# A projection's products with the high halves of the weights all issued ahead of those with the low halves

## The chip, the cores and the metric

The kernel runs on one core of one Trainium2 chip. The metric is device time in microseconds (us) of one execution. The three runs of the kernel before took 1165.89, 1167.34 and 1170.15 us, so the median is 1167.34 us.

## What is computed

The reference chains two transformer-like blocks over 256 tokens of width 1024, in float32. Cut to what matters here:

```python
# first block: 16 meta tokens + 256 tokens
proj = rms_norm(h) @ w_in                    # attention, RWKV and gate columns
merged = sigmoid(gate_sb) * (y_sb @ w_sb_out) + sigmoid(gate_rw) * (y_rw @ w_rw_out)
h = h + merged @ w_out
gate_ffn, up_ffn = split(rms_norm(h) @ w_ffn_in)       # 2 x 2816 columns
h = h + (silu(gate_ffn) * up_ffn) @ w_ffn_out
# second block
mod = silu(c) @ w_ada + b_ada                # shifts, scales and gates
proj = modulated(h) @ w_in_2                 # gated delta rule, HGRN2, gates
x = x + g1 * (concat(oA, oB) @ w_out_2)
x = x + g2 * moe(modulated(x))               # 64 experts, 8 of them for each token
```

All the products with `w_in`, `w_sb_out`, `w_rw_out`, `w_out`, `w_ffn_in`, `w_ffn_out`, `w_in_2` and `w_out_2` are called projections below.

## The kernel before

**Weights.** The weights of the projections are cut into tiles of 128x128 numbers and laid out in the order in which they are used. Eight tiles make a unit (`UNIT = 8`); there are 168 units, counted here from 0. `unit` (L270 to L280) loads a unit by one DMA of 512 KB on SP's queue into a `raw` buffer, and `split` (L322 to L326) then makes two tiles of it: ScalarE (ACT) writes the high half `whi`, a copy in the matmul's reduced float32 (L324), and VectorE (DVE) or, for the 30 units listed in `POOLU`, GpSimd (POOL) subtracts it from `raw` to give the low half `wlo` (L325). The three kinds of tile have three buffers each. `wt` (L285 to L292) hands out one tile's two halves and calls for the unit after it as well (`AHEAD = 1`).

**Products.** The activations are kept as a high and a low half too. Each weight tile takes part in three matmuls that add up in one PSUM tile: high by high, high by low, and low weight by high activation. Every matmul has 256 columns (272 where the meta tokens are included). So a unit has 24 products, 16 of them with `whi` and 8 with `wlo`. `mm3` (L328 to L332) issues the three one behind another; `linear` (L334 to L339) does so for the `kt` tiles of one output tile `m`. `pair` (L341 to L359) holds two output tiles in one PSUM tile and writes the three matmuls out (L352, L357, L358); ffn_in's 22 pairs come from it. `linears` (L361 to L369) with `by_k` takes several output tiles together, one activation tile `k` after another, so that PE can begin while the activations still arrive: the first three tiles of the program (`rw_lo`), the first two of `w_out` (`EARLYM = 2`) and the first two of the second block (`k2`). `mix_half` (L1380 to L1396) does the second output projection.

**Order.** Stages are Python generators whose turns are written in strings of letters (`FIRST`, `MIXER`), and ffn_out (`residual`, L987) advances the loads of `w_ada` (`ada`) between its tiles; these are loaded by SP into `wada` buffers and summed on DVE (L1086). A list scheduler then places the instructions on each engine's queue by dependencies, buffers and its own estimates. Each queue runs in its written order. From about 780 us to the end the kernel runs the experts, with a schedule written by hand in which the projections' code has no part.

**Stages in time.** Up to 330 us: the first block's projections, recurrences, attention, mixing and `w_out` (about 300 us). 330 to 460 us: ffn_in. 460 to 545 us: ffn_out, 8 output tiles of 22 weight tiles each. 545 to about 750 us: the second block's projections and recurrences: the convolution and decay work of the gated delta rule (L1208, L1209, L1217, L1223), the scans of HGRN2 (L1270, L1274), the inverse of the delta rule (`base_inverse`, L393 and L394). Then the router and the experts.

Of the kernel before, what the change touches and what calls it, by code (L numbers as in the profile page):

```python
# [40 lines left out]
UNIT = 8  # L41
# [168 lines left out]
class Ker:  # L210
# [117 lines left out]
    def mm3(self, out, w, x, start, stop):  # L328
# [2 lines left out]
        mm(out, w[0], x[1], start=False, stop=False)  # L331
        mm(out, w[1], x[0], start=False, stop=stop)  # L332

    def linear(self, block, m, kt, x, n, tag="mm"):  # L334

        p = self.psum(tag)
        for k in range(kt):
            self.mm3(p[:, :n], self.wt(block, m * kt + k), x(k), k == 0, k == kt - 1)
        return p[:, :n]  # L339

    def pair(self, block, parts, kt, x, by_k=False):  # L341

        p = self.psum().rearrange("p (a b) -> p a b", b=S)
        steps = [(i, m, k) for i, (m, ks) in enumerate(parts) for k in ks]
        if by_k:
            steps.sort(key=lambda t: t[2])
        mm = self.nc.tensor.matmul
        for n, (i, m, k) in enumerate(steps):
            w, v = self.wt(block, m * kt + k), x(k)
            last = k == parts[i][1][-1]  # L350
            kw = dict(skip_group_check=True)
            a = mm(p[:, i], w[0], v[0], start=(n == 0), stop=False, **kw)  # L352
            if n == 0:
                first = a
            elif k == parts[i][1][0]:
                self.order(a, first)
            mm(p[:, i], w[0], v[1], start=False, stop=False, **kw)  # L357
            mm(p[:, i], w[1], v[0], start=False, stop=last, **kw)  # L358
        return p  # L359

    def linears(self, block, ms, kt, x, n, by_k, tag="mm"):  # L361

        if not by_k:
            return [self.linear(block, m, kt, x, n, tag) for m in ms]
        ps = [self.psum(tag)[:, :n] for _ in ms]
        for k in range(kt):
            for p, m in zip(ps, ms):
                self.mm3(p, self.wt(block, m * kt + k), x(k), k == 0, k == kt - 1)
        return ps  # L369

    def rsqrt(self, out, src, scale, eps, tmp):
# [1008 lines left out]
    def mix_half(self, c):  # L1380

        if not c:
            self.pmix = [self.psum("ax") for _ in range(3)] + [self.psum("mm")]
        yh, yl = self.ymix2
        for m in range(KD):
            p = self.pmix[m // 2][:, m % 2 * S:m % 2 * S + S]
            for k in range(4):
                w = self.wt("w_out2" + "ab"[c], 4 * m + k)
                x = (yh[:, 4 * c + k], yl[:, 4 * c + k])
                mm = self.nc.tensor.matmul  # L1390
                kw = dict(skip_group_check=True)
                mm(p, w[0], x[0], start=(c == 0 and k == 0 and m % 2 == 0), stop=False, **kw)
                mm(p, w[0], x[1], start=False, stop=False, **kw)
                mm(p, w[1], x[0], start=False, stop=(c == 1 and k == 3), **kw)
            if c:
                yield m, p  # L1396

# [782 lines left out]
```

## Time and profile before

| | before |
|---|---|
| three runs | 1165.89, 1167.34, 1170.15 us |
| median | 1167.34 us |
| the profiled execution | 1175.33 us |
| its span | 1173.5 us |
| mean granted TensorE clock | 0.959 of full speed |
| PE busy | 1086.6 us, 93% of the span |
| DVE busy | 682.1 us, 58% |
| ACT busy | 436.8 us, 37% |
| POOL busy | 243.0 us, 21% |

The profiled execution is 8.0 us (0.7%) longer than the median of the runs; its span, from the first to the last instruction that the profile records, is 1.8 us shorter than its own time. PE's 93% is an average over stages with different limits: between 330 and 460 us PE hardly pauses, in the stages before and after it waits for other engines, and from 780 us on it runs beside a DMA stream that is always full. "Idle before" in a row is the time for which the engine stood still ahead of the instruction, and the arrow names what ended that.

### The profile page before, as it was taken

To read this page: it belongs to the slowest core of one execution; us is meant where nothing else is said; L and a number is where in the kernel's file an instruction comes from. 1 tells how busy PE (TensorE), PEld (TensorE's weight loads), DVE (VectorE), ACT (ScalarE), POOL (GpSimd) and SP (SyncE) were. 2 spreads that over 40 slices of the span, in tenths; PEclk is the share of its full clock that TensorE was granted. 3 is DMA by queue.
4 is the path that set the end of the run, shared out by engine and by line. 5 is a ranking of instruction groups with operands and counts; after the bars stand their busy time and mean duration, and the time that the engine had idled before them with its cause. 6 is when DMAs were issued, how large, how long until landed. Compare 5 with 4: busy or idle time off the path is not lost.

```text
span 1173.5 us, 20361 instructions
## 1 busy us (share of the span) xinstructions
PE 1086.6 (93%) x8038; PEld 831.6 (71%) x8038; DVE 682.1 (58%) x1211; ACT 436.8 (37%) x707; POOL 243.0 (21%) x245
## 2 busy tenths in 40 slices
PE   5989899999989999988988999899999999999994
PEld 4889787789979999877988889773444444444441
DVE  5598633346678888877799888522233333333333
ACT  5744433365454444335854645411111111111112
POOL 1261102023312000486472131410000000000000
PEclk9899969999989999998999999799999999999998
DMA  5455511024558898864443504959999999999993
GB/s 174 141 145 176 177 55 37 1 86 166 179 198 298 314 341 302 306 232 145 148 146 127 176 28 174 415 182 344 418 413 392 419 419 419 399 419 418 420 418 139
DMA packets 67495, 290.69 MB, mean 248 GB/s; under 512 B 15984, under 2 KB 17136, under 8 KB 46912
## 3 DMA queue, kind: packets, MB, share of 16 engines
q1 hardware_dynamic: 66528, 287.93, 65.5%
q8 instruction: 66, 1.08, 0.4%
q10 hardware_dynamic: 864, 1.38, 0.3%
q14 instruction: 37, 0.30, 0.1%
HBM read 285.77 MB, written 3.51 MB: 247 GB/s over the span
## 4 chain that ended last, share of the span: by engine, by line
PE 45%; DMA 16%; DVE 11%; issue 4%; ACT 4%; POOL 3%; SPq 0%; POOLq 0%; ACTq 0%; DVEq 0%
DMA er<-in_E_dram 10%; PE bank L1880 10%; PE bank L1908 5%; PE p_b L357 3%; PE p_b L358 3%; PE p_b L352 3%; DMA wada<-in_W_ada_dram 3%; PE acc L1777 3%; PE bank L1840 3%; DMA xa<-in_E_dram 3%; DVE wada L1086 2%; DVE wlo L325 2%; PE p_b L787 2%; ACT k L306 2%; PE p_b L332 2%
## 5 line engine op out<-in xcount | busy, mean ns | idle before, releaser
L324 ACT ACTIVATE whi<-raw 128x1024 fp32r<-128x1024 f32 x168 | 175.5, 1055 | 102.7 <-PE p_b L331 37.0
L325 DVE TENSOR_TENSOR wlo<-raw,whi 128x1024 fp32r<-128x1024 f32 x138 | 178.4, 1299 | 59.5 <-ACT whi L324 55.4
L358 PE MATMUL p_b<-k,wlo 128*128 128x256 f32 x608 | 175.7, 290 | 4.9 <-DVE wlo L325 3.0
L352 PE MATMUL p_b<-k,whi 128*128 128x256 f32 x608 | 176.1, 290 | 3.5 <-ACT k L324 2.3
L357 PE MATMUL p_b<-k,whi 128*128 128x256 f32 x608 | 176.1, 290 | 2.3 <-DVE k L325 2.3
L332 PE MATMUL p_b<-k,wlo 128*128 128x256 f32 (+2 forms) x496 | 144.6, 296 | 13.1 <-DVE wlo L325 9.0
L330 PE MATMUL p_b<-k,whi 128*128 128x256 f32 (+2 forms) x496 | 146.8, 300 | 9.3 <-ACT k L324 4.1
L331 PE MATMUL p_b<-k,whi 128*128 128x256 f32 (+2 forms) x432 | 126.8, 296 | 0.3 <-DVE k L1114 0.3
L358 PEld LDWEIGHTS p_b<-k,wlo 128*128 128x128 f32 x608 | 118.6, 195 | 8.3 <-DVE wlo L325 4.0
L352 PEld LDWEIGHTS p_b<-k,whi 128*128 128x128 f32 x608 | 118.8, 196 | 5.1 <-ACT k L324 2.4
L325 POOL TENSOR_TENSOR wlo<-raw,whi 128x1024 fp32r<-128x1024 f32 x30 | 81.6, 2723 | 196.7 <-ACT whi L324 136.5
L357 PEld LDWEIGHTS p_b<-k,whi 128*128 128x128 f32 x608 | 118.8, 196 | 3.8 <-DVE k L325 2.8
L332 PEld LDWEIGHTS p_b<-k,wlo 128*128 128x128 f32 (+1 forms) x496 | 97.1, 198 | 15.8 <-DVE wlo L325 10.9
L330 PEld LDWEIGHTS p_b<-k,whi 128*128 128x128 f32 (+1 forms) x496 | 97.4, 198 | 14.6 <-ACT k L324 5.1
L1880 PE MATMUL bank<-er,x 128*32 128x512 f32 (+2 forms) x464 | 91.9, 612 | 2.6 <-DMA er<-in_E_dram 2.5
L1908 PE MATMUL bank<-er,k 128*32 128x512 f32 (+2 forms) x488 | 89.9, 595 | 2.6 <-DMA er<-in_E_dram 1.4
L1880 PE MATMUL bank<-er,h 128*32 128x512 f32 (+2 forms) x488 | 87.5, 595 | 0.0
L1828 POOL TENSOR_TENSOR k<-k,masks 128x128 f32<-128x128 f32 (+3 forms) x44 | 17.3, 423 | 335.7 <-DVE y L325 310.8
L331 PEld LDWEIGHTS p_b<-k,whi 128*128 128x128 f32 (+1 forms) x432 | 85.7, 199 | 0.8 <-DVE k L1114 0.6
L1086 DVE SCALAR_TENSOR_TENSOR wada<-wada,crow 128x1024 f32<-128x1024 f32 x48 | 70.9, 1484 | 21.7 <-DMA wada<-in_W_ada_dram 21.6
L1885 ACT ACTIVATE k<-bank 128x256 f32<-128x256 f32 x24 | 9.2, 384 | 195.7 <-PE bank L1880 195.7
L1886 DVE SCALAR_TENSOR_TENSOR k<-k,gs,bank 128x256 f32<-128x256 f32 x24 | 11.5, 481 | 101.9 <-ACT k L1885 101.9
(476 smaller groups left out, 2043.5 us busy)
## 6 DMA issues: line engine op xcount, KB each, us to landing
er<-in_E_dram SPq DMA_DIRECT2D x132, 1024.0 KB, 17.7
raw<-in_W_dram SPq DMA_DIRECT2D x168, 512.0 KB, 3.9
wada<-in_W_ada_dram SPq DMA_DIRECT2D x48, 512.0 KB, 5.5
xa<-in_E_dram SPq DMA_DIRECT2D x24, 1024.0 KB, 12.5
xa<-in_Sh_dram SPq DMA_DIRECT2D x2, 1024.0 KB, 8.3
k<-in_xT_dram SPq DMA_DIRECT2D x4, 272.0 KB, 4.7
dl<-x SPq DMA_DIRECT2D x1, 1024.0 KB
x<-in_xT_dram SPq DMA_DIRECT2D x1, 1024.0 KB
```

The costliest lines, as they stand in the source:

```text
L324: ins = self.nc.scalar.activation(hi, src, AF.Copy)
L325: (engine or self.nc.vector).tensor_tensor(lo, src, hi.bitcast(F32), op=OP.subtract)
L330: mm(out, w[0], x[0], start=start, stop=False)
L331: mm(out, w[0], x[1], start=False, stop=False)
L332: mm(out, w[1], x[0], start=False, stop=stop)
L352: a = mm(p[:, i], w[0], v[0], start=(n == 0), stop=False, **kw)
L357: mm(p[:, i], w[0], v[1], start=False, stop=False, **kw)
L358: mm(p[:, i], w[1], v[0], start=False, stop=last, **kw)
L1086: nc.vector.scalar_tensor_tensor(w, w, 1.0, c, op0=OP.mult, op1=OP.mult, accum_out=self.mod[:, o:o + 1])
L1777: self.nc.tensor.matmul(self.acc[t], w, x, start=t not in self.started, stop=False, skip_group_check=True)
L1880: mm(ph[t], X[:, k, i * 128 + t.start:i * 128 + t.stop], u[:, kk * 512:kk * 512 + 512], start=(k == 0), stop=(k == KD - 1), skip_group_che ...
L1908: nc.tensor.matmul(py[t], q.H[:, k, t], u[:, k * 1024 + c * 512:k * 1024 + c * 512 + 512], start=(k == 0), stop=(k == 1), skip_group_check ...
```

## The change

Within a run of tiles, all the products with `whi` are written first and all the products with `wlo` behind them. A new helper `three` does that for a list of terms. `by_unit` cuts an output tile's `kt` weight tiles at the borders of units, so that in `linear` a run is at most one unit. In `pair` a run is one of the two output tiles (8 weight tiles), or, with `by_k`, both of them together. In `linears` with `by_k` one run holds all the tiles of all the outputs. In `mix_half` a run is 4 tiles. `mm3` stays for the small products outside. No product, load, split or buffer is added or taken away; PE has as many instructions as before. The list scheduler works on the changed program, so the queues of DVE, ACT, POOL and SP differ from before here and there as well.

```diff
+    def three(self, terms, **kw):
+        mm = self.nc.tensor.matmul
+        for out, w, x, start, _ in terms:
+            mm(out, w[0], x[0], start=start, stop=False, **kw)
+            mm(out, w[0], x[1], start=False, stop=False, **kw)
+        for out, w, x, _, stop in terms:
+            mm(out, w[1], x[0], start=False, stop=stop, **kw)
+
+    def by_unit(self, block, tiles):
+        runs = []
+        for t in tiles:
+            u = (self.off[block] + t) // UNIT
+            if not runs or runs[-1][0] != u:
+                runs.append((u, []))
+            runs[-1][1].append(t)
+        return [r for _, r in runs]
+
     def linear(self, block, m, kt, x, n, tag="mm"):
-        p = self.psum(tag)
-        for k in range(kt):
-            self.mm3(p[:, :n], self.wt(block, m * kt + k), x(k), k == 0, k == kt - 1)
-        return p[:, :n]
+        p = self.psum(tag)[:, :n]
+        for run in self.by_unit(block, range(m * kt, m * kt + kt)):
+            self.three([(p, self.wt(block, t), x(t - m * kt), t == m * kt, t == m * kt + kt - 1) for t in run])
+        return p
...
     def pair(self, block, parts, kt, x, by_k=False):
...
+        groups = [steps] if by_k else [[s for s in steps if s[0] == i] for i in range(len(parts))]
...
+        for g in groups:
+            for i, m, k in g:
...
+                mm(p[:, i], w[0], v[1], start=False, stop=False, **kw)
+            for i, m, k in g:
+                w, v = self.wt(block, m * kt + k), x(k)
+                mm(p[:, i], w[1], v[0], start=False, stop=k == parts[i][1][-1], **kw)
...
     def linears(self, block, ms, kt, x, n, by_k, tag="mm"):
...
-        for k in range(kt):
-            for p, m in zip(ps, ms):
-                self.mm3(p, self.wt(block, m * kt + k), x(k), k == 0, k == kt - 1)
+        self.three([(p, self.wt(block, m * kt + k), x(k), k == 0, k == kt - 1) for k in range(kt) for p, m in zip(ps, ms)])
```

**ffn_out, PE, around unit 116.** PE's queue before, in one of ffn_out's output tiles: `whi_5225` and `wlo_5226` are unit 116's halves, `whi_5195` and `wlo_5196` those of unit 115, and `hid_3320` and `hid_3321` the activations' high and low halves.

```order
L330 MATMUL p_b3_5260<-hid_3320,whi_5195 128x256
L331 MATMUL p_b3_5260<-hid_3321,whi_5195 128x256
L332 MATMUL p_b3_5260<-hid_3320,wlo_5196 128x256
L330 MATMUL p_b3_5260<-hid_3320,whi_5225 128x256
L331 MATMUL p_b3_5260<-hid_3321,whi_5225 128x256
L332 MATMUL p_b3_5260<-hid_3320,wlo_5226 128x256
```

The same place after the change:

```order
L339 MATMUL p_b3_5260<-hid_3320,whi_5225 128x256
L340 MATMUL p_b3_5260<-hid_3321,whi_5225 128x256
L342 MATMUL p_b3_5260<-hid_3320,wlo_5226 128x256 x8
L339 MATMUL p_b3_5260<-hid_3320,whi_5275 128x256
L340 MATMUL p_b3_5260<-hid_3321,whi_5275 128x256
```

Before, unit 116's first `wlo` product stood behind two of its `whi` products. Now it stands behind 16 of them.

**ffn_out, DVE, unit 107.** DVE's queue before; `wlo_4897` is unit 107's low half, L1086 sums one 512 KB piece of `w_ada`:

```order
L1055 TENSOR_SCALAR k1_4848<-k1_4848 128x8
L325 TENSOR_TENSOR hid_3321<-k1_4839,hid_3320 128x256
L1086 SCALAR_TENSOR_TENSOR wada_5244,mod_2669<-wada_5244,crow_3389 128x1024
L325 TENSOR_TENSOR wlo_4897<-raw_4894,whi_4896 128x1024
L325 TENSOR_TENSOR wlo_4927<-raw_4924,whi_4926 128x1024
L1086 SCALAR_TENSOR_TENSOR wada_5247,mod_2669<-wada_5247,crow_3389 128x1024
L1086 SCALAR_TENSOR_TENSOR wada_5250,mod_2669<-wada_5250,crow_3389 128x1024
```

And after the change:

```order
L1077 TENSOR_SCALAR k1_4848<-k1_4848 128x8
L325 TENSOR_TENSOR hid_3321<-k1_4839,hid_3320 128x256
L325 TENSOR_TENSOR wlo_4897<-raw_4894,whi_4896 128x1024
L1108 SCALAR_TENSOR_TENSOR wada_5244,mod_2669<-wada_5244,crow_3389 128x1024
L325 TENSOR_TENSOR wlo_4927<-raw_4924,whi_4926 128x1024
L1108 SCALAR_TENSOR_TENSOR wada_5247,mod_2669<-wada_5247,crow_3389 128x1024
L1018 TENSOR_TENSOR x1_79<-p_b3_4851,x1_79 128x256
```

The split of unit 107 now stands ahead of a sum over `w_ada`, and unit 108's ahead of another, where before one sum stood ahead of both.

**Second block, DVE and PE, unit 138.** DVE's queue before, where `wlo_6244` and `wlo_6279` are the low halves of units 138 and 139:

```order
L1208 TENSOR_SCALAR k2_6082<-p_b5_6077,k1_6071 128x128
L1209 TENSOR_SCALAR k2_6083<-p_b5_6077,k1_6071 128x128
L325 TENSOR_TENSOR wlo_6244<-raw_6241,whi_6243 128x1024
L325 TENSOR_TENSOR wlo_6279<-raw_6276,whi_6278 128x1024
L1223 SCALAR_TENSOR_TENSOR k4_6067<-p_b7_6096,k1_6009,k2_6082 128x128 x4
L1208 TENSOR_SCALAR k2_6158<-p_b5_6153,k1_6147 128x128
L1209 TENSOR_SCALAR k2_6159<-p_b5_6153,k1_6147 128x128
```

After the change (L1230, L1231, L1245, L1292 and L1296 are the old L1208, L1209, L1223, L1270 and L1274):

```order
L1230 TENSOR_SCALAR k2_6158<-p_b5_6153,k1_6147 128x128
L1231 TENSOR_SCALAR k2_6159<-p_b5_6153,k1_6147 128x128
L1292 SCALAR_TENSOR_TENSOR k4_6188<-k1_6184,k4_5913 128x256 x4
L325 TENSOR_TENSOR wlo_6244<-raw_6241,whi_6243 128x1024
L1245 SCALAR_TENSOR_TENSOR k4_6067<-p_b7_6174,k1_6009,k2_6158 128x128 x4
L1296 TENSOR_TENSOR k4_5916<-k4_5916,p_b4_6193 128x256
L1296 TENSOR_TENSOR k4_5916<-k4_5916,p_b0_6228 128x256
L325 TENSOR_TENSOR wlo_6279<-raw_6276,whi_6278 128x1024
```

The split of unit 138 has moved from ahead of four L1223 to behind them, behind eight of L1208 and L1209, and behind the four scans. PE's queue at that unit after the change (`whi_6278` is unit 139's high half):

```order
L339 MATMUL p_b3_6333<-k8_5668,whi_6278 128x256
L340 MATMUL p_b3_6333<-k8_5669,whi_6278 128x256
L342 MATMUL p_b1_6263<-k8_5668,wlo_6244 128x256 x4
L342 MATMUL p_b2_6298<-k8_5668,wlo_6244 128x256 x4
L339 MATMUL p_b2_6298<-k8_5668,whi_6278 128x256
```

Ahead of these rows stand the 16 `whi` products of unit 138, so that its first `wlo` product, which before followed two products of the unit, now follows 24 products with `whi`: 16 of its own and 8 of unit 139, which were moved ahead of it.

## Rows read from the trace of the kernel before

**Rows 1.** The page: busy time, share of the span and instructions of PE

```profile
PE 1086.6 (93%) x8038; PEld 831.6 (71%) x8038; DVE 682.1 (58%) x1211; ACT 436.8 (37%) x707; POOL 243.0 (21%) x245
```

**Rows 2.** PE's waits over the span: engine, line, awaited, us in total, times, longest

```profile
PE p_b L332 <- DVE wlo L325: 11.7, 11, 2.5
PE p_b L332 <- POOL wlo L325: 10.8, 5, 3.4
...
PE p_b L358 <- DVE wlo L325: 3.0, 4, 1.7
...
PE p_b L358 <- POOL wlo L325: 1.9, 1, 1.9
```

**Rows 3.** PE's waits in 0:150 (first row), 460:545 (two), 600:665 (two)

```profile
PE p_b L332 <- DVE wlo L325: 4.9, 5, 1.9
...
PE p_b L332 <- POOL wlo L325: 6.7, 3, 3.4
PE p_b L332 <- DVE wlo L325: 2.7, 2, 1.5
...
PE p_b L332 <- POOL wlo L325: 4.0, 2, 2.4
PE p_b L332 <- DVE wlo L325: 3.4, 3, 2.5
```

**Rows 4.** Windows: us, busy of PE, PEld, DVE, ACT, POOL, clock, DMA share, GB/s

```profile
60.00:120.00 60.00, 56.13 (x453) 53.90 (x452) 54.12 (x92) 25.92 (x36) 22.82 (x16) 1.00 0.56 164
460.00:545.00 85.00, 71.32 (x571) 68.91 (x569) 67.17 (x80) 32.32 (x43) 46.56 (x30) 0.96 0.74 258
600.00:665.00 65.00, 55.76 (x434) 54.10 (x433) 63.98 (x126) 35.39 (x47) 22.53 (x13) 0.95 0.46 143
```

**Rows 5.** The page: groups, with busy time and mean ns of one

```profile
L325 DVE TENSOR_TENSOR wlo<-raw,whi 128x1024 fp32r<-128x1024 f32 x138 | 178.4, 1299 | 59.5 <-ACT whi L324 55.4
...
L325 POOL TENSOR_TENSOR wlo<-raw,whi 128x1024 fp32r<-128x1024 f32 x30 | 81.6, 2723 | 196.7 <-ACT whi L324 136.5
```

**Rows 6.** Timeline of PE around 505 us: start, duration, engine, line; idle before

```profile
505.24 0.58 PE L332 MATMUL p_b<-hid,wlo 128*128 128x256 f32 x1 [3.41 <-POOL wlo L325]
505.62 0.41 PE L330 MATMUL p_b<-hid,whi 128*128 128x256 f32 x1
...
508.16 0.28 PE L330 MATMUL p_b<-hid,whi 128*128 128x256 f32 x1
508.28 0.28 PE L331 MATMUL p_b<-hid,whi 128*128 128x256 f32 x1
```

**Rows 7.** Timeline of PE: two more long waits, at 361 and 523 us

```profile
360.95 0.39 PE L358 MATMUL p_b<-k,wlo 128*128 128x256 f32 x1 [1.91 <-POOL wlo L325]
...
361.46 0.42 PE L358 MATMUL p_b<-k,wlo 128*128 128x256 f32 x1
...
523.22 0.39 PE L332 MATMUL p_b<-hid,wlo 128*128 128x256 f32 x1 [2.35 <-POOL wlo L325]
523.45 0.28 PE L330 MATMUL p_b<-hid,whi 128*128 128x256 f32 x1
```

**Rows 8.** Timeline of PE: the early tiles of w_out and k2, last activations

```profile
306.17 0.39 PE L330 MATMUL p_b<-k,whi 128*128 128x256 f32 x1 [1.12 <-ACT k L324]
...
307.33 0.28 PE L330 MATMUL p_b<-k,whi 128*128 128x256 f32 x1
...
553.07 0.35 PE L331 MATMUL p_b<-k,whi 128*128 128x256 f32 x1
```

**Rows 9.** Timeline of DVE (three rows) and PE (one) around unit 138

```profile
583.80 2.35 DVE L325 TENSOR_TENSOR wlo<-raw,whi 128x1024 fp32r<-128x1024 f32 x2
587.33 1.13 DVE L1223 SCALAR_TENSOR_TENSOR k<-p_b,k,k 128x128 f32<-128x128 f32 x4 [1.18 <-POOL k L1217]
...
590.44 4.49 DVE L1270 TENSOR_TENSOR_SCAN k<-k,k 128x256 f32<-128x256 f32 x3
...
587.50 0.28 PE L330 MATMUL p_b<-k,whi 128*128 128x256 f32 x1
```

More of the change, by code (lines that the diff above doesn't have):

```diff
@@ L332, in mm3 @@
         mm(out, w[1], x[0], start=False, stop=stop)
+    def three(self, terms, **kw):
[13 more added lines that the diff above has]
+        return [r for _, r in runs]
     def linear(self, block, m, kt, x, n, tag="mm"):
-        p = self.psum(tag)
-        for k in range(kt):
-            self.mm3(p[:, :n], self.wt(block, m * kt + k), x(k), k == 0, k == kt - 1)
-        return p[:, :n]
+        p = self.psum(tag)[:, :n]
+        for run in self.by_unit(block, range(m * kt, m * kt + kt)):
+            self.three([(p, self.wt(block, t), x(t - m * kt), t == m * kt, t == m * kt + kt - 1) for t in run])
+        return p
     def pair(self, block, parts, kt, x, by_k=False):
         p = self.psum().rearrange("p (a b) -> p a b", b=S)
+        mm = self.nc.tensor.matmul
+        kw = dict(skip_group_check=True)
         steps = [(i, m, k) for i, (m, ks) in enumerate(parts) for k in ks]
@@ L346, in pair @@
             steps.sort(key=lambda t: t[2])
[L347 to L358, printed above, removed]
+        groups = [steps] if by_k else [[s for s in steps if s[0] == i] for i in range(len(parts))]
+        first = None
+        for g in groups:
+            for i, m, k in g:
+                w, v = self.wt(block, m * kt + k), x(k)
+                a = mm(p[:, i], w[0], v[0], start=first is None, stop=False, **kw)
+                if first is None:
+                    first = a
+                elif k == parts[i][1][0]:
+                    self.order(a, first)
+                mm(p[:, i], w[0], v[1], start=False, stop=False, **kw)
+            for i, m, k in g:
+                w, v = self.wt(block, m * kt + k), x(k)
+                mm(p[:, i], w[1], v[0], start=False, stop=k == parts[i][1][-1], **kw)
         return p
@@ L1386, in mix_half @@
             p = self.pmix[m // 2][:, m % 2 * S:m % 2 * S + S]
[L1387 to L1394, printed above, removed]
+            self.three([(p, self.wt("w_out2" + "ab"[c], 4 * m + k), (yh[:, 4 * c + k], yl[:, 4 * c + k]),
+                         c == 0 and k == 0 and m % 2 == 0, c == 1 and k == 3) for k in range(4)], skip_group_check=True)
             if c:
```

## The prediction

> **What bounds the kernel now.** I read the page's busy times first: PE works for 1086.6 us, 93% of the span [rows 1], so a change that only reorders PE's instructions can gain no more than what PE stands still for. The view of PE's waits shows how much of that belongs to the low halves of the weights: 11.7 us in 11 waits and 10.8 us in 5 at L332, 3.0 us in 4 and 1.9 us in 1 at L358 [rows 2], together 27.4 us in 21 waits, 2.3% of the time. Cut by stretch, the larger parts are 4.9 us before 150 us, 6.7 + 2.7 = 9.4 us in ffn_out (460 to 545 us), and 4.0 + 3.4 us between 600 and 665 us [rows 3]. Then the windows, which tell whether PE's wait is the one that ends last there. In ffn_out nobody is full: in 85 us DVE works for 67.2, POOL for 46.6, and the DMA engines for 0.74 of the time. From 600 to 665 us DVE works for 64.0 of 65 us, so PE's waits are DVE's shadow; from 60 to 120 us it works for 54.1 of 60 [rows 4]. From about 780 us on nothing of the change is executed: what is gained before shifts the experts forward as a block.
>
> Why PE waits is seen in one timeline. At 505.24 us the wait of 3.41 us ends at a product with `wlo`, and a product with `whi` follows at once, 0.38 us later [rows 6]: it needed only what was there, and stood in the queue behind the low half. The queue as printed ahead of this text shows that two `whi` products of unit 116 came before it. The low half is ready late because it is the last of a chain, with 1.30 us for DVE's subtraction and 2.72 us for POOL's [rows 5].
>
> **The change, part by part.**
>
> *Cover.* In a run of eight tiles 16 products now precede the first `wlo` one, 14 more than before. At 0.12 us from one start to the next (508.16 to 508.28 [rows 6]) that is 14 x 0.12 = 1.68 us; every wait loses what it has up to that.
>
> *ffn_out.* The three waits on POOL are 3.41 us [rows 6], 2.35 us [rows 7] and the rest of 6.7, 0.99 us; the first two keep 1.73 and 0.67 us. So 9.4 - 2.4 = **7.0 us** go. One unit, 107, serves an output tile with two of its tiles only and has little cover; its split was moved ahead of a sum over `w_ada` on DVE, as the queue shows, and I count it as covered by that. The upper bound is all 9.4 us; the lower is 3.5 us, if SP's loads, which were placed anew among those of `w_ada`, bring back half. I take 7.0 because DVE, POOL and DMA each have a fifth of the stretch or more to spare [rows 4].
>
> *ffn_in.* The one long wait, 1.91 us at 360.95 us [rows 7], loses 1.68: **1.7 us**; PE is the fullest engine there.
>
> *Before 150 us.* 4.9 us at L332 [rows 3] bound it above. DVE is 90% busy from 60 to 120 us [rows 4], and an inverse with a long chain on DVE ends what follows; below, nothing. I take half, **2.5 us**: the rows give DVE a tenth of the time to spare, so neither end is near.
>
> *600 to 665 us.* **Nothing**, for want of a free DVE. Were that cover gone, up to 7.4 us would come back.
>
> *The clock.* After the 3.41 us wait a product lasts 0.41 us where it lasts 0.28 from 508.16 us on; twelve products start between 505.62 and 508.16 us, 0.21 us apart, and then again 0.12 [rows 6]. So 12 x 0.09 = 1.1 us went to the lower of the two clocks (1.2 GHz). A wait of 1.91 us at 360.95 was followed by the lower clock too (0.42 us for the product at 361.46); one of 2.35 us at 523.22 was not, as the next product's 0.28 us tells [rows 7]. Both lowered clocks should be kept up when the waits shrink to 1.7 and 0.2 us: **2.2 us**, with 0 and 2.2 as its ends. The Trainium skill, "TensorE: Matmul & The Clock Gate", section "Loop structure matters more than you think", blames the drop on a long wait between matmuls; read so, only the longest of these waits gives clock back, and the forecast would stand 1.1 us higher. The row at 360.95 us speaks against so strict a reading, and I go by it.
>
> *Runs by `by_k`: a cost.* In the first two tiles of `w_out` the last activation came at 306.17 us, after a wait of 1.12 us, and the next output tile began at 307.33 us [rows 8]. With eight activations and two output tiles, 16 `wlo` products now stand behind it all, where two did: 14 x 0.12 = 1.7 us of work that used to fill the gaps between the activations comes after them. The first pair of k2, whose last activation came at about 553.07 us [rows 8], is the same, and its output feeds the convolution. Each costs 0 (if the deferred products fill gaps further on) to 1.7 us; I take 1.5 each, being near the row with a real wait: **-3.0 us**. For the first three tiles of the program and ffn_in's first pair I take nothing: there the products run behind the activations at the lower clock, so PE has work anyway; at most 1.7 us each.
>
> *DVE's queue at unit 138: a cost.* Before, the splits of units 138 and 139 ran from 583.80 us for 2.35 us, in time that DVE would have lost waiting for POOL until 587.33 us (a wait of 1.18 us remained) [rows 9]. Now 138's is behind that wait, four L1223 (1.13 us), eight L1208 and L1209 (until 590.44 us) and four scans, three of which took 4.49 us [rows 9]. At 1.5 us a scan that is 590.4 + 6.0 + 1.2 = 597.6 us at the latest, and 594 to 595 if the scans run at their fastest. PE comes to the unit at 587.50 us [rows 9] and has 24 `whi` products first, 2.9 us: it will stand still from 590.4 for about 4 to 7 us. What this costs the end is less, since from 600 us on DVE is what ends last: DVE loses the 2.35 us of work that lay in its wait. Between 0 and 7 us I take **-2.35 us**.
>
> *ACT, POOL and SP* issue what they issued before, a high half here or there earlier; nothing, since none of them is near full in any stretch of [rows 4].
>
> **Sum.** 7.0 + 1.7 + 2.5 + 2.2 - 3.0 - 2.35 = 8.05 us. Against the profiled execution, 1175.3 us, that gives 1167.3; it stands 8.0 us above the median of the runs, and on the median I forecast 1167.3 - 8.0 = **1159.3 us**, 0.7% less.
>
> **Rivals.**
>
> *The waits only move.* The low halves come no sooner; where DVE is the limit PE meets them later and as long. Then the early 2.5 us stay out, ffn_out keeps 5 us, only the clock of the 505 us wait comes back (1.1), and unit 138 costs PE its full 7 us: 5 + 1.7 + 1.1 - 3.0 - 7 = -2.2, so 1169.5; with half that cost, 1166. For it speaks DVE's 64.0 of 65 us [rows 4]; against it, that ffn_out, where most of the waiting is, has no full engine. Some 1163 to 1171 us.
>
> *All of it comes back.* If the reordering lets DVE start its chain sooner, the 4.9 us before 150 us and the 7.4 us after 600 us return as well, and unit 138 costs nothing: 8.05 + 2.4 + 7.4 + 2.35 = 20.2 us, 1147 us. Against it: the full DVE.
>
> *Slower: the scheduler defers the splits.* It places a split by when it thinks the low half is needed, and that is now later. On a full DVE a deferred split is a wait of PE's like the 7 us at unit 138. One such unit is already in the sum; it turns the sign when two more of the same price are not absorbed (8.05 - 14 = -6): 1173 us, and 1180 with three. The place is the second block, 580 to 665 us, where splits, scans and the inverse share DVE. Against it: the queues elsewhere show splits moved ahead as often as back.
>
> That the change does nothing is ruled out for PE's order, which is visibly other; it could do nothing for the time, which is the first rival.
>
> **How the numbers follow.** A change of 0.5%, 5.8 us, is about what a measurement of this kernel can tell from none, so faster means below 1161.5 and slower above 1173.2 us. The forecast (1154 to 1164 us) gets 0.47, the first rival 0.30, the full return 0.12, the slower one 0.11. Of the forecast's 0.47, 0.39 lies below 1161.5 us; with the full return that makes 0.51 for faster. The other 0.08 and 0.28 of the first rival give 0.36 for no difference; the slower rival and the upper edge of the first, 0.02, give 0.13 for slower. The range goes from 1149 to 1171 us: below it most of the full return is left out, above it the slower rival.
>
> **What would show it.** In the changed profile: PE's waits for `wlo` in ffn_out down from 9.4 to about 2.4 us, in ffn_in near nothing; no lower clock right behind 361 and 505 us (on the new time axis); a new wait of PE of 4 to 7 us at the first `wlo` product of unit 138; two tails of 16 `wlo` products each with a DVE or POOL consumer behind it; DVE still full between 600 and 665 us with PE's waits of some 7 us left. The experts' stage should begin about 8 us earlier and last as long as before. I am wrong if the waits in ffn_out reappear under another name (the high half, or a load), if the second block takes 5 us or more longer than before, or if the early stages give back nothing.

## The result, and the profile after

The changed kernel takes 1183.42 us, median of 4 runs (1179.35 to 1187.19); the kernel before, run beside it, 1168.74 us (1165.89 to 1172.12, 4 runs). The ratio on record is 1.0115, with a 95% interval of 1.0085 to 1.0144: **slower by 1.2%**. The medians lie 14.7 us apart, and 1159.3 us was forecast. The profiled execution took 1182.09 us with a span of 1180.4 us, 1.3 us below its median; that of before stood 6.6 us above the median of these runs, so the two traces differ by 6.8 us only, and the rest of the 14.7 lies between executions of one kernel. In the experiments below one execution of e2 took 5812.84 us and is left out of its figures.

The busy times of the changed kernel's page answer to [rows 1]: no engine has more work, PE has 2.5 us more of it, and it stands still for 91.3 us of the span instead of 86.9 us.

```profile
PE 1089.1 (92%) x8038; PEld 831.5 (70%) x8038; DVE 681.6 (58%) x1211; ACT 438.7 (37%) x707; POOL 240.8 (20%) x245
```

PE's waits over the span (engine, line, awaited, us in total, times, longest), for [rows 2]; L339 and L342 are the old L330 and L332, L382 the old L358.

```profile
PE p_b L342 <- POOL wlo L325: 10.5, 4, 4.0
PE p_b L342 <- DVE wlo L325: 9.8, 7, 4.8
...
PE p_b L339 <- ACT whi L324: 2.9, 4, 1.1
...
PE p_b L382 <- DVE wlo L325: 0.8, 3, 0.4
```

The waits for low halves have gone from 27.4 us in 21 to 21.1 us in 14, so 6.3 us are given back by this view. Those for high halves have grown, from 1.1 us to 3.5 (L339 and L374), so 3.9 us are left. The same view by stretch answers to [rows 3]. The stretches 0 to 150 us (one row), 450 to 535 us, which holds ffn_out (three), and 535 to 665 us (two); the 0.8 us at L382 are all in ffn_in, between 330 and 450 us:

```profile
PE p_b L342 <- DVE wlo L325: 2.2, 2, 2.0
...
PE p_b L342 <- POOL wlo L325: 6.7, 2, 4.0
PE p_b L339 <- ACT whi L324: 1.5, 2, 1.1
PE p_b L342 <- DVE wlo L325: 1.0, 2, 0.6
...
PE p_b L342 <- DVE wlo L325: 6.6, 3, 4.8
PE p_b L342 <- POOL wlo L325: 3.8, 2, 2.5
```

Early the waits are halved. In ffn_out 7.7 of 9.4 us are left, and 1.5 us for high halves have come with them. In the second block they are no smaller: 10.4 us, where before had 9.8 between 545 and 665 us (the 7.4 us of [rows 3], 1.7 us at L358 and 0.7 us more at L332).

Where the time went is seen by following one product through both traces: when PE executes the last low-half product of a unit, less the time of the same product in before, in us (minus is ahead). It is worked out from the timelines of PE, one profiled execution of each kernel (for the other rows see the experiments). That of e9 stood 7.3 us below the median of its runs.

```
unit                    51     75    133    139    156    161
changed kernel       -12.5  -12.0   -8.9   -0.2   -2.6   +6.9
splits_first (e3)    -12.3  -10.5   -9.5   -7.7   -7.5   +9.4
gates2_old (e4)      -14.8  -14.2  -14.7   -6.7   -7.5   -7.5
new_pinned (e9)      -20.4  -19.0  -15.2  -15.2  -14.3  -11.3
old_pinned (e10)      -2.0   -2.5   +0.4  +11.0  +10.4  +16.8
second_old (e11)     -12.6  -12.1   -7.3   -7.1   -7.1   -7.0
```

The changed kernel enters the second block (unit 133) 8.9 us ahead and is 6.9 us behind at unit 161, in the block's last projection: it loses 15.8 us, 6.3 of them up to unit 156 and 9.5 behind it. Between units 133 and 139 alone it loses 8.7 us, of which some come back up to unit 156. The experts' stage passes the 6.9 us on unchanged. Not all of the 8.9 us is the change's doing: in before's profiled execution the clock was granted at half for 10.2 us between 42 and 54 us, which the changed kernel did not meet in its own; that is some 5 us (an estimate, half of the 10.2).

Look at the part up to unit 156 first. From 600 us on DVE is the fullest engine there (63.56 of 65 us), as in before ([rows 4]). The windows from the end of unit 127's split to the end of unit 156's (columns as in [rows 4]), of before:

```profile
537.50:657.30 119.80, 103.27 (x794) 98.66 (x794) 108.13 (x210) 76.33 (x134) 58.91 (x52) 0.94 0.42 134
```

and of the changed kernel:

```profile
527.90:656.10 128.20, 109.29 (x815) 103.60 (x814) 109.04 (x210) 77.96 (x135) 53.57 (x52) 0.92 0.37 125
```

The same 210 instructions of DVE, 0.9 us more of work, but 8.4 us more of time: DVE is idle for 128.20 - 109.04 = 19.2 us instead of 11.7. What it waits for is another list. DVE's longest waits in these stretches, of before:

```profile
DVE k L1198 <- PE p_b L1195: 4.0, 2, 3.0
DVE k L1223 <- POOL k L1217: 1.2, 1, 1.2
DVE k L1138 <- ACT k L306: 1.1, 1, 1.1
DVE wlo L325 <- ACT whi L324: 1.1, 1, 1.1
```

and of the changed kernel (22 is added to a line number of this part of before):

```profile
DVE wlo L325 <- ACT whi L324: 4.0, 4, 1.6
DVE k L1195 <- ACT k L306: 2.7, 1, 2.7
DVE k L1245 <- POOL k L1239: 2.4, 2, 1.8
DVE k L1296 <- ACT k L306: 2.2, 1, 2.2
```

Before, DVE waited mostly for a product of PE; now for ACT, 8.9 us in the six waits shown, and for POOL. The wait of 2.7 us shows how. L1195 belongs to the small tile (4x256) from which the decay of the delta rule comes, and on which the whole inverse rests. The timeline of DVE:

```profile
564.59 0.60 DVE L1195 SCALAR_TENSOR_TENSOR k<-k,k 4x256 f32<-4x256 f32 x1 [2.75 <-ACT k L306]
```

and that of ACT ahead of it:

```profile
559.52 1.06 ACT L324 ACTIVATE whi<-raw 128x1024 fp32r<-128x1024 f32 x1
560.48 0.64 ACT L306 ACTIVATE k<-p_b 128x256 f32<-128x256 f32 x2
561.01 1.34 ACT L306 ACTIVATE k<-k 128x256 f32<-128x256 f32 x4
562.24 0.65 ACT L306 ACTIVATE k<-p_b 128x256 f32<-128x256 f32 x2
562.77 1.79 ACT L306 ACTIVATE k<-k 128x256 f32<-128x256 f32 x5
```

The last of the five at 562.77 us is what L1195 needs; ahead of it ACT works off twelve activations of 128x256 for `fiq2`, among them those of the scans, which DVE comes to at 580.96 us. In before the same small activation stands right behind one high half:

```profile
566.53 1.06 ACT L324 ACTIVATE whi<-raw 128x1024 fp32r<-128x1024 f32 x1
567.62 0.42 ACT L306 ACTIVATE k<-k 4x256 f32<-4x256 f32 x1
```

so that DVE, busy with a split until 568.85 us, took its result without a wait, at 568.88 us. The wait lies on the chain of work that ended last, the path on which each piece released the next. Rows of that chain (start, duration, engine, line), three of the changed kernel, then one of before:

```profile
560.58 3.54 ACT k L306 x12
564.14 0.42 ACT k L306
564.59 0.61 DVE k L1195
...
569.12 5.30 ACT k L306 x18
```

In before the long row of activations follows the small one of 567.62 us; in the changed kernel twelve of them precede it. On average ACT is 61% busy in the stretch (77.96 of 128.20 us), but just here it hardly pauses: 19.00 of the 20 us from 555 to 575 us, and in before 22.87 of the 23 us from 562 to 585 us:

```profile
562.00:585.00 23.00, 21.50 (x171) 20.16 (x171) 16.14 (x30) 22.87 (x49) 6.52 (x12) 1.00 0.44 141
```

So in this part of the block the order of ACT's queue decides whose result is late. The one wait does not make the whole loss, though: it stands with 2.8 us in the profiles of e3 and e4 too, and e4 takes no longer than before.

The last 9.5 us (unit 156 to unit 161, +6.9 less -2.6) fall between 656 and 720 us. There the granted clock falls, which in before it didn't between 628 and 725 us. Windows of the changed kernel:

```profile
664.00:667.00 3.00, 2.21 (x11) 2.21 (x12) 2.81 (x5) 1.58 (x3) 1.64 (x2) 0.68 0.42 63
...
679.00:688.00 9.00, 9.00 (x45) 6.17 (x44) 3.54 (x4) 2.74 (x5) 3.98 (x4) 0.50 0.16 58
```

From 679 to 688 us PE runs at 1.2 GHz (0.50) without a gap. The first fall comes with a wait of 2.76 us for POOL at 664.79 us; ahead of the second PE waited 0.47 us at the most, and executed matmuls of 32x32.

### The profile page after: what moved, and what is told of

Its sections match the earlier page's. It is cut to its first block, busy times and chain, and to the rows that moved or that the text cites. A ratio compares the mean times of both kernels' runs of the same rounds, so it can differ in the third digit from the quotient of the medians.

```text
span 1180.4 us, 20362 instructions
## 1 busy us (share of the span) xinstructions
PE 1089.1 (92%) x8038; PEld 831.5 (70%) x8038; DVE 681.6 (58%) x1211; ACT 438.7 (37%) x707; POOL 240.8 (20%) x245
## 4 chain that ended last, share of the span: by engine, by line
PE 38%; DMA 18%; DVE 12%; POOL 4%; ACT 4%; issue 3%; SPq 0%; POOLq 0%; ACTq 0%; DVEq 0%
DMA er<-in_E_dram 11%; PE bank L1896 9%; DMA wada<-in_W_ada_dram 4%; PE bank L1924 4%; PE acc L1793 3%; DVE wlo L325 3%; PE bank L1856 3%; PE p_b L379 3%; PE p_b L374 2%; PE p_b L382 2%; PE p_b L342 2%; PE p_b L339 2%; PE p_b L340 2%; DMA xa<-in_E_dram 2%; DVE wada L1108 2%
## 5 line engine op out<-in xcount | busy, mean ns | idle before, releaser
L374 PE MATMUL p_b<-k,whi 128*128 128x256 f32 x608 | 154.0, 289 | 3.4 <-ACT k L324 2.3
L379 PE MATMUL p_b<-k,whi 128*128 128x256 f32 x608 | 153.5, 288 | 2.1 <-DVE k L325 1.9
L339 PE MATMUL p_b<-k,whi 128*128 128x256 f32 (+1 forms) x480 | 127.5, 297 | 11.9 <-ACT k L324 5.3
L374 PEld LDWEIGHTS p_b<-k,whi 128*128 128x128 f32 x608 | 117.2, 193 | 7.1 <-ACT k L324 2.4
L379 PEld LDWEIGHTS p_b<-k,whi 128*128 128x128 f32 x608 | 117.3, 193 | 3.7 <-DVE k L325 2.8
L340 PE MATMUL p_b<-k,whi 128*128 128x256 f32 (+1 forms) x416 | 109.6, 295 | 0.4 <-DVE k L1136 0.3
L339 PEld LDWEIGHTS p_b<-k,whi 128*128 128x128 f32 x480 | 95.1, 200 | 15.1 <-ACT k L324 6.6
L1108 DVE SCALAR_TENSOR_TENSOR wada<-wada,crow 128x1024 f32<-128x1024 f32 x48 | 77.7, 1623 | 27.6 <-DMA wada<-in_W_ada_dram 27.6
L342 PE MATMUL p_b<-k,wlo 128*128 128x256 f32 (+1 forms) x480 | 80.7, 297 | 12.6 <-DVE wlo L325 8.8
L382 PE MATMUL p_b<-k,wlo 128*128 128x256 f32 x608 | 90.3, 285 | 0.8 <-DVE wlo L325 0.8
L340 PEld LDWEIGHTS p_b<-k,whi 128*128 128x128 f32 x416 | 82.2, 199 | 1.1 <-DVE k L1136 0.6
L382 PEld LDWEIGHTS p_b<-k,wlo 128*128 128x128 f32 x608 | 79.8, 190 | 2.6 <-DVE wlo L325 1.7
L342 PEld LDWEIGHTS p_b<-k,wlo 128*128 128x128 f32 x480 | 69.2, 200 | 14.5 <-DVE wlo L325 10.0
```

The source lines that it names most:

```text
L339: mm(out, w[0], x[0], start=start, stop=False, **kw)
L340: mm(out, w[0], x[1], start=False, stop=False, **kw)
L342: mm(out, w[1], x[0], start=False, stop=stop, **kw)
L374: a = mm(p[:, i], w[0], v[0], start=first is None, stop=False, **kw)
L382: mm(p[:, i], w[1], v[0], start=False, stop=k == parts[i][1][-1], **kw)
L1108: nc.vector.scalar_tensor_tensor(w, w, 1.0, c, op0=OP.mult, op1=OP.mult, accum_out=self.mod[:, o:o + 1])
```

## The experiments

The whole program of the change is kept or undone by block. All kernels that do so have this in common, with another set of blocks in `old`:

```diff
+    def old(self, block):
+        return block in ("k2", "ba2", "fiq2", "qv2", "gates2", "w_out2", "w_out2a", "w_out2b")
...
         runs = self.by_unit(block, range(m * kt, m * kt + kt))
+        if self.old(block):
+            runs = [[t] for t in range(m * kt, m * kt + kt)]
...
+        if self.old(block):
+            groups = [[s] for s in steps]
```

**Which half of the program loses.** second_old (e2) has the new order up to ffn_out and the old one in the second block, as in the diff:

> The change up to ffn_out; every projection of the second block in the old order. Theory A (the second block's own new order loses what is lost there): the block begins 8 to 9 us earlier than in the kernel before and lasts as long as before: about 1160 us. Theory B (the second block takes back whatever comes early): about 1168 us, as before.

Measured: 1159.31 us, the median of three executions (1154.19 to 1161.13); ratio 0.9881 [0.9819, 0.9943]: faster. The loss sits in the second block, the gain ahead of it. Its mirror, old up to ffn_out and new behind (e6):

```diff
-        return block in ("k2", "ba2", "fiq2", "qv2", "gates2", "w_out2", "w_out2a", "w_out2b")
+        return block not in ("k2", "ba2", "fiq2", "qv2", "gates2", "w_out2", "w_out2a", "w_out2b")
```

> The old order up to ffn_out, the new one in the second block alone. Theory A (what the second block loses it loses by its own order, by late splits and the lowered clock): the kernel before plus some 15 us, 1182 to 1187 us. Theory B (it loses only what came early from before it): no slower than before, 1168 to 1171 us.

Measured: 1189.17 us (4 runs), 1.0149 [1.0113, 1.0186], no faster than the whole change, whose interval it meets, and 2 us above the range of theory A. As e2's runs had a high mean clock (0.976 in the profile), it was run again in more rounds (e11, the same kernel):

> The change up to ffn_out, the old order in the second block, once more and in more rounds, since the first time only three of its executions counted. If the gain of the first part is real, 1158 to 1163 us beside about 1170 for the kernel before, a ratio of 0.988 to 0.993; if the first time was a lucky draw of the clock's stretches, above 0.993.

Measured: 1166.83 us (12 runs), 0.9952 [0.9927, 0.9978]. By its expectation e2's 0.988 was a lucky draw. This is the figure to keep: the new order up to ffn_out is worth 0.5%, 4.9 us. In its trace a lead of 7.3 us at unit 133 is still 7.0 us at unit 161.

**The first block.** Two kernels ask what is left there. e1 is the whole change with the old order in `w_out` alone:

```diff
+    def old_k(self, block):
+        return block == "w_out"
...
+        if self.old(block) or self.old_k(block):
+            for k in range(kt):
+                for p, m in zip(ps, ms):
+                    self.three([(p, self.wt(block, m * kt + k), x(k), k == 0, k == kt - 1)])
```

> The change, but the two early output tiles of w_out (linears with by_k) keep the old order of products; PE's queue differs there alone, DVE's nowhere. Theory A (the 16 deferred wlo products make PE wait between activations and drop its clock, 5.1 us lost between units 51 and 55): PE is 5 us earlier at unit 55 than in the change, and the whole is 5 us shorter, about 1178 us. Theory B (what is gained before the second block is handed on to a wait there): earlier at unit 55, but the whole stays at 1183 us.

Measured: 1180.84 us (10 runs), 1.0069 [1.0032, 1.0106]; the interval meets that of the change, so the time is unclear on it. In the traces the changed kernel loses 5.1 us from unit 51 to 55, e1 3.5 us, so the tail costs some 1.6 us. The 5 us that were expected did not come: most of that loss is there with the old order of `w_out` too. The same with the second block old as well (e5, e2 and e1 in one):

> The change up to ffn_out only, and there the two early tiles of w_out in the old order as well. Theory A (the 16 deferred products of w_out cost 1.6 us, what the pair of runs before showed between the last activation and the next output tile): 1 to 2 us less than with the new order there, 1158 to 1159 us. Theory B (the activations bound that place, whatever PE does): the same 1160 us.

Measured: 1165.54 us (4 runs), 0.9954 [0.9919, 0.9989]. Both theories were reckoned from e2's time and missed; it is the same as e11: a tail of 1.6 us is too little to be told from nothing by the times.

e8 asks what the waits that are left in ffn_out are. In the changed kernel PE waits 3.99 us for the low half of unit 115. PE's timeline there:

```profile
490.74 1.02 PE L342 MATMUL p_b<-hid,wlo 128*128 128x256 f32 x4 [3.99 <-POOL wlo L325]
```

and that of POOL, which splits it:

```profile
486.68 0.73 POOL L1024 TENSOR_TENSOR k<-k,k 128x256 f32<-128x256 f32 x1 [6.61 <-DVE k L1080]
487.36 3.33 POOL L325 TENSOR_TENSOR wlo<-raw,whi 128x1024 fp32r<-128x1024 f32 x1
```

POOL stood still for 6.61 us with the split queued behind L1024, which waits for an output tile that PE reaches later now. Unit 121's split (511.03 us) stands behind work of the same kind. e8 is e2 with these two units split by DVE:

```diff
-POOLU = (17, 18, 26, 29, 36, 42, 46, 51, 65, 68, 69, 72, 94, 105, 109, 111, 112, 115, 116, 117, 119, 120, 121, 140, 143, 145, 149, 151, 158, 161)
+POOLU = (17, 18, 26, 29, 36, 42, 46, 51, 65, 68, 69, 72, 94, 105, 109, 111, 112, 116, 117, 119, 120, 140, 143, 145, 149, 151, 158, 161)
```

> The change up to ffn_out only, with the splits of units 115 and 121 on DVE in place of POOL. Theory A (PE's waits of 3.7 and 2.8 us for them are POOL's queue, where the split of 115 stands behind a product of an output tile that PE has yet to finish): both waits fall below 1 us, 3 to 6 us less, 1154 to 1157 us. Theory B (DVE has the sums over w_ada, late by DMA, ahead of them): the waits come back on DVE, 1160 us.

Measured: 1162.4 us (4 runs), 0.9902 [0.9854, 0.995], which can't be told from e11: theory B rather than A. PE's waits for both halves in ffn_out are 7.4 us in e11's profile, which has the two units on POOL, and 6.7 us here. The rows of e8:

```profile
PE p_b L348 <- DVE wlo L325: 3.0, 3, 1.5
PE p_b L345 <- ACT whi L324: 2.4, 3, 1.6
PE p_b L348 <- POOL wlo L325: 1.3, 3, 0.6
```

Those for POOL fall from 6.9 us in e11 to 1.3 us, and those for ACT and DVE rise from 0.5 to 5.4 us: most of the wait only takes another name.

**Is it the splits?** The slower rival said that deferred splits on DVE do it. e3 is the whole change with the splits of units 138 and 139 put ahead of the first L1245 on DVE, where they stood before:

```diff
+            if u in (138, 139):
+                self.order(self.behind, self.lo_ins)
...
+                if b == h == 0:
+                    self.behind = ins
```

> The change, and on DVE the splits of units 138 and 139 are held ahead of the four L1245 and the scans, as in the kernel before. Theory A (the place of these splits costs about 8 us between units 134 and 139): PE waits for them no more, unit 139 ends 5 to 8 us earlier than in the change; the whole is 3 to 8 us shorter, 1175 to 1180 us. Theory B (DVE, full after 600 us, is what counts): unit 139 earlier, but from unit 144 on as in the change, 1182 to 1184 us.

Measured: 1187.65 us (4 runs), 1.0137 [1.0091, 1.0183]: no better. In the trace the first half of theory A came true: unit 139 is 7.7 us ahead of before and not 0.2, and unit 156 still 7.5 us. It is lost again behind, 16.9 us up to unit 161, where the clock was granted at half for 24 us between 656 and 720 us (13.6 us in the changed kernel). e4 is the whole change with the old order in `gates2` alone, the block whose products run beside the inverse:

> The change, but gates2's pairs in the old order. Theory A (the old order left products of gates2 between the small matmuls of the inverse from 664 to 690 us and so kept the clock up): no lowered clock in that stretch, 7 to 9 us less, about 1175 us. Theory B (the clock falls after the 2.76 us wait for POOL at 664.8 us, whatever gates2 does): the lowered clock stays, about 1183 us.

Measured: 1172.11 us (10 runs), 1.0002 [0.9973, 1.0032]: it recovers 11 us, more than theory A had. Its clock stays full from 660 to 690 us and it loses nothing from unit 156 on. Up to 641 us its DVE, ACT and POOL execute the change's instructions in the change's order, and up to unit 156 it loses 7.2 us as the change loses 6.3; DVE is idle for 127.10 - 109.03 = 18.1 us:

```profile
522.70:649.80 127.10, 105.53 (x792) 99.36 (x792) 109.03 (x211) 77.25 (x134) 53.57 (x52) 0.93 0.40 128
```

So the idle DVE costs 6 to 7 us, which the gain up to ffn_out about makes up for, and the larger part of the change's loss is made behind unit 156. e7 is e4 and e3 in one kernel:

> The change with two repairs: gates2 in the old order, and the splits of units 138 and 139 held ahead of the four L1245 and the scans on DVE. Theory A (late splits cost 3 us at unit 156, hidden in the run with that repair alone by the lowered clock behind it): 3 us less than with gates2 old alone, about 1169 us. Theory B (DVE, full after 600 us, takes it back): 1172 us.

Measured: 1184.73 us (4 runs), 1.0109 [1.0067, 1.0152], above both theories. From unit 133 to 139 it loses 1.8 us where e4 loses 8.0, then 4.0 up to unit 156 and 8.9 behind it; the clock fell again, with `gates2` old as in e4. So with the two splits early most of the loss up to unit 139 is gone, but not the time: neither their place nor the order within `gates2` explains it by itself, and each such edit lets the scheduler place all queues anew. That led to the theory that the queues are the cause.

**Products and queues apart.** In e9 PE has the whole change, and the instructions of DVE, ACT and POOL that the second block issues are held in before's order by an edge of issue order from each to the next (`PIN` lists the ranks; no wait is added across engines):

```diff
+    def pin(self):
+        traced = self.nc.cur_bb.bb.instructions[self.n0:]
+        for name, ranks in self.PIN.items():
+            mine = [i for i in traced if i.engine == getattr(mybir.EngineType, name)]
+            queue = [mine[int(k)] for k in ranks.split()]
+            for a, b in zip(queue, queue[1:]):
+                self.tc.add_manual_dep(b, a.name, mybir.DependencyInfo(mybir.DependencyClass.NoSync, mybir.DependencyReason.DATA), reason="pin")
```

> The whole change on PE, but in the second block the queues of DVE, ACT and POOL are held in the order that they have in the kernel before; the scheduler is free with PE and SP alone. Theory A (the loss comes from the queues that the scheduler placed anew, which leave DVE idle 7 to 8 us more): DVE's idle time between the splits of units 127 and 156 goes back from 19.2 to about 12 us, the lowered clock from 664 to 690 us is gone, and the whole takes 1155 to 1162 us. Theory B (PE's new order in itself brings the results that DVE waits for later): DVE still idles 17 us or more, 1172 us or more.

Measured: 1172.03 us (10 runs), 0.9999 [0.9963, 1.0036]. The time of theory A (1155 to 1162 us) was missed and lies where B had it, but DVE's idle time is A's; the lowered clock is short (665 to 668.5 us), not gone. The window of the same stretch as above:

```profile
521.30:643.10 121.80, 107.63 (x821) 102.72 (x819) 108.41 (x211) 77.13 (x135) 57.56 (x52) 0.94 0.41 133
```

DVE is idle for 13.4 us, near before's 11.7, and it waits for PE again as it did before (L1234 is before's L1198):

```profile
DVE wlo L325 <- ACT whi L324: 4.9, 5, 1.2
DVE k L1234 <- PE p_b L1231: 3.2, 2, 2.5
```

e10 is the reverse: PE has the old order of products everywhere, and DVE, ACT and POOL are held in the second block to the queues of the changed kernel, by the same `pin` with other ranks.

> The old order of the products everywhere, and in the second block the queues of DVE, ACT and POOL held in the order that the change has there. Theory A (those queues are the loss): DVE idles 17 us or more between the splits of units 127 and 156, and the whole is 7 us (without a lowered clock behind it) to 16 us (with one) slower than the kernel before, 1175 to 1186 us. Theory B (PE's new order is the loss): as the kernel before, 1168 to 1172 us.

Measured: 1189.4 us (4 runs), 1.018 [1.0137, 1.0223], above the range of theory A and as slow as the change or slower (the intervals just meet). Each product's three matmuls are written as in before. The window, with DVE idle for 22.8 us:

```profile
537.00:668.00 131.00, 107.81 (x799) 101.66 (x798) 108.16 (x210) 77.87 (x134) 53.20 (x52) 0.92 0.39 124
```

and DVE's waits, the same list as the changed kernel's (L1187, L1237 and L1288 are its L1195, L1245 and L1296):

```profile
DVE wlo L325 <- ACT whi L324: 4.9, 5, 1.8
DVE k L1288 <- ACT k L306: 3.5, 1, 3.5
DVE k L1187 <- ACT k L306: 2.8, 1, 2.8
DVE k L1237 <- POOL k L1231: 2.4, 2, 1.8
```

Side by side, ratio to before and its interval:

```
second block:            queues of before            queues of the change
first block new
  products old           0.9952 [0.9927, 0.9978] e11     -
  products new           0.9999 [0.9963, 1.0036] e9  1.0115 [1.0085, 1.0144] the change
first block old
  products old           1                           1.0180 [1.0137, 1.0223] e10
  products new               -                       1.0149 [1.0113, 1.0186] e6
```

The queues cost 1.2% in one pair (the change against e9) and 1.8% in the other (e10 against before); the order of products in the second block costs 0.5% with before's queues (e9 against e11, whose intervals just don't part) and nothing with the new ones (e6 against e10). e6's queues were not held, but in its trace DVE, ACT and POOL execute the second block in the change's order, instruction by instruction. PE's queue was not held in any of them, and the scheduler fitted it to the queues that it was given: in e10 at least 254 of PE's 8038 matmuls stand where before has another, in e9 at least 191 where the change has another. So the cost is that of the three queues together with the places that PE's products then took; the two are not parted.

e12 is e9 with DVE's queue held alone, ACT's and POOL's left to the scheduler:

> The whole change on PE, and in the second block DVE's queue alone held as in the kernel before; ACT and POOL as the scheduler likes. Theory A (DVE's own order is what starves it): DVE idles 12 to 14 us between the splits of units 127 and 156, and the time is that of the run with three queues held, 1168 to 1174 us. Theory B (ACT and POOL, placed anew, hand DVE its inputs late): DVE idles 17 us or more and the time stays near the change's, 1178 us or more.

Measured: 1181.7 us (7 runs), 1.0078 [1.0046, 1.0109]; DVE is idle for 124.20 - 107.69 = 16.5 us:

```profile
530.50:654.70 124.20, 106.18 (x805) 100.80 (x803) 107.69 (x211) 76.46 (x135) 55.75 (x52) 0.93 0.40 129
```

The time is theory B's, and the idle time lies just under B's 17 us; but the interval meets the change's, so DVE's own order is at most a part of it. With that order given, it waits for the others' (L1207 and L1257 are the changed kernel's L1195 and L1245):

```profile
DVE k L1207 <- ACT k L306: 4.3, 1, 4.3
DVE wlo L325 <- ACT whi L324: 3.8, 2, 2.6
DVE k L1257 <- POOL k L1251: 3.5, 1, 3.5
```

That the three queues have to come from one schedule is the likely reading; with one kernel for it, it is not shown.

The version to keep is that of e11, the new order up to ffn_out and the old one behind: 0.9952 in 12 runs, below before and below the change.

## Why the prediction was wrong

**What failed** are two steps, one place: "*ACT, POOL and SP* issue what they issued before, a high half here or there earlier; nothing, since none of them is near full in any stretch of [rows 4]", and "600 to 665 us. Nothing", with "DVE's queue at unit 138" at -2.35 us as the one cost. The forecast took the other engines' queues in the second block as those of before but for one spot. The scheduler had placed all three anew. The traces show DVE idle 7.5 us longer, mostly for ACT and POOL, and then 9.5 us lost from 656 to 720 us. By the table of pairs the queues are about 1.16% of the 1.63% between e11 and the change (13.6 of 19 us; 1.8% by the other pair) and PE's own order about 0.47% (5.5 us).

The reason given for the nothing was a gap in the rows: [rows 4] have no window between 545 and 600 us, and there ACT worked for 22.87 of 23 us in before (562 to 585 us). An average of 61% over the block hides it. And that an engine has time to spare says that it can do its work, not that it does the right piece first. The order of ACT's instructions was to be had before the run, as DVE's was, and it was not read against DVE's needs.

**The spot at unit 138** was priced from the wrong rows. PE waited 0.53 us there, not 4 to 7. PE's timeline (unit 138, then unit 140):

```profile
584.55 1.22 PE L342 MATMUL p_b<-k,wlo 128*128 128x256 f32 x8 [0.53 <-DVE wlo L325]
...
591.42 2.72 PE L342 MATMUL p_b<-k,wlo 128*128 128x256 f32 x11 [2.45 <-POOL wlo L325]
```

and DVE's:

```profile
580.96 2.43 DVE L1292 TENSOR_TENSOR_SCAN k<-k,k 128x256 f32<-128x256 f32 x4
583.30 1.20 DVE L325 TENSOR_TENSOR wlo<-raw,whi 128x1024 fp32r<-128x1024 f32 x1
```

The scans came before the second set of L1245, not behind it, and four of them took 2.43 us where 6.0 was reckoned from three at 4.49 us [rows 9]. The stalls of the second block lie elsewhere, at units 140 and 144 (2.45 and 4.8 us).

**ffn_out, 7.0 us**: wrong. 9.4 us of waits became 7.7, and 1.5 us for high halves came with it, so 0.2 us were gained by this view (2.0 in e11's profile). That is one of the forecast's own signs of being wrong, waits that reappear for the high half; the other is the second block, longer by 15.8 us. A cover of 14 products was counted on splits that stay where they were; the two on POOL did not (units 115 and 121), because POOL's queue holds work that waits for a tile of PE's. "SP's loads", named as the risk, were not it: PE's longest wait for a high half there (1.07 us at 509.57 us) ends with a split that stands on ACT behind 6.44 us of waiting for DVE (L1027). In the sum the third wait on POOL is 0.94 us, not 0.99, which changes nothing.

**ffn_in, 1.7 us, and before 150 us, 2.5 us**: right. Of the waits at L358 (3.0 and 1.9 us [rows 2]) 2.5 us lay in ffn_in, and 0.8 are left; before 150 us 4.9 us at L332 became 2.2 us. The forecast did not place the rest of L358: 0.8 us lay before 150 us and 1.7 between 600 and 665 us, where it counted 7.4 us and not 9.1.

**The clock, 2.2 us**: it did not come. At the old 361 us no long wait and no lower clock are left. In ffn_out the wait has moved to unit 115, and behind it a product lasts 0.41 us as it did in [rows 6]; and behind unit 121, whose wait left the clock up in before, it is granted at half from 515 to 518 us. So the lower clock comes twice, as often as before at 361 and 505 us.

**The tails by `by_k`, 1.5 us each**: right in `w_out` by single executions (1.6 us); the times don't tell it from nothing, and that of k2 wasn't measured apart.

For these steps up to ffn_out the forecast makes 7.0 + 1.7 + 2.5 + 2.2 - 1.5 = 11.9 us, and e11 measured 4.9 us (2.6 to 8.6 by its interval). The mis-sized terms are ffn_out and the clock, 9.2 us together.

**The rivals.** The slower one had the sign, the place (580 to 665 us) and the agent, the scheduler, at 1173 to 1180 us; it had a part of the pieces. It spoke of splits that are deferred on a full DVE; e3 and e7, which pull two of them forward, lose 1.8 us up to unit 139 and not 8 to 9, but gained no time, and DVE's own order, held alone, is a part at most (e12). That "the waits only move" is near what ffn_out shows (9.4 us before, 9.2 with the high halves). For the second block, where a full DVE would swallow the lead, it is refuted by e2, e5, e8 and e11: with the queues of before, a lead passes through the second block and loses 0 to 1.4 us.

**What stays open** is the stretch from 656 to 720 us. The lower clock there came in the profiles of all kernels with the new order in the second block but e4's, and in none with the old order throughout it, e10's short one (0.61 from 676 to 680 us) excepted, which has the new queues. What is lost from unit 156 to 161 goes with it, though not one to one: 16.9 us with 24 us of lower clock in e3, 9.5 with 13.6 in the changed kernel, 6.4 with 3.4 in e10, 3.0 with 3.4 in e9, nothing in e4 and e11, where the clock stays up. At half the clock PE does in 13.6 us what takes it 6.8 us at the full one, so by itself the clock explains at most 6.8 of the 9.5 us (an estimate from the 13.6 us). What lets the clock fall, and how much of the 9.5 us is clock and how much the queues, these runs don't part. Nor was a kernel run with ACT's or POOL's queue held alone, or with PE's held as well.

## What to carry to other kernels

An edit to one engine's order also lets a list scheduler place the queues of the others anew, so compare the order on every engine that feeds the bound one in each stage, and read it against what that engine needs next; an engine at 60% on average can be full just where it matters, and then its order decides who is late. To find out whether the order or the queues cost the time, run the new order with the old queues and the old order with the new queues: two kernels parted here what edits of single spots (e3, e4, e7) did not. And keep such a change to the stages where it pays.

## What the runs showed of the hardware

The same instructions in the same order drift apart with the clock. Up to unit 35, where the changed kernel, e1, e2, e4, e7 and e9 issue the same, their profiles stand between -6.0 and -16.5 us against before, in the order of the time for which the clock was granted at half before 180 us: none in e2 (-16.5), 3.4 us in e9 (-15.3), 17 us in e4 and e7 (-9.7 and -9.6), 20 us in the changed kernel (-7.7), 31 us in e1 (-6.0). One profile of each is too few to read a difference of a few us; the mean clock of a run goes with its time, loosely (58 runs of before: 1171.9 us and 0.965 in the mean, some 6 us less time for 0.01 more clock, with a correlation of -0.6).

A scan of 128x256 on DVE took about 0.6 us in the changed kernel (four in 2.43 us, POOL standing still), and 1.5 us in before (three in 4.49 us [rows 9], POOL at work until 594.38 us); before's fourth, at 595.87 us with POOL standing still, took 0.68 us.
